# A 31-tap depthwise convolution: from VectorE to TensorE, 4 taps x 32 channels in the rows, 4 groups in the columns

## The chip, the cores and the metric

One core of a Trainium2 chip runs the whole program in one launch. The metric is the time of one execution on the device, in microseconds (us). The kernel before takes 3641.28 us (median of 3 runs, 3637.17 to 3642.21).

## The reference, cut to what matters

Two layers (`DEPTH = 2`) work on 1024 latent and 256 context tokens of width 1024. In each, one input projection feeds four mixers of 256 channels: a recurrence (RG-LRU), attention, a convolution module and hyena, a pair of long convolutions. One output projection joins them, and a mixture of 32 experts follows. In the last layer context tokens feed only the recurrence and the attention, so the convolution module runs on 1280 tokens in layer 0 and on 1024 in layer 1. The convolution module is:

```
def conformer_conv(pc, conv_w, conv_b, ln_g, ln_b, w_pw, b_pw):
    u = pc[..., :W_C] * jax.nn.sigmoid(pc[..., W_C:])               # W_C = 256 channels
    u = dwconv(u, conv_w, conv_b, (CONF_K // 2, CONF_K // 2))       # CONF_K = 31 taps, one filter per channel
    u = layer_norm(u, ln_g, ln_b)
    return jax.nn.silu(u) @ w_pw + b_pw
```

`dwconv` is depthwise: output channel c at time t is the sum over j of w[j, c] u[t + j - 15, c], plus a bias. All of it is in float32.

## The kernel before

Every layer has the same stages. What bears on this change is in two of them.

**Stage 1 (`phase1`).** Channels lie on the 128 partitions, tokens along the row. `win` makes one block of 128 projected columns: 24 products of 128 x 512 (or 256) per group of tokens, from a high and a low part of weights and inputs (L1065). The weights come over one buffer `wir` and are split by ScalarE (L948) and GpSimd (L951). The order is: the input of the first half of the recurrence, the recurrence on it (`recur(0)`), the two blocks of the convolution module (`glu_evac`), the recurrence's gate, `recur(1)`, then queries, keys and values, and the second gate. The recurrence goes piece by piece, 6 pieces for each half: GpSimd and VectorE make a 4-tap convolution `rg_u` (L1399, then three instructions of L1401), TensorE two products from it (L1404, four instructions), ScalarE, VectorE and GpSimd the gates, and VectorE a scan (L1421, L1424). `rg_u` has one buffer, so a piece starts when the one before has let it go (L1411).

Queries and keys leave as high and low parts: `qk_evac` issues 4 stores for each of 12 tiles in layer 0 (fewer in layer 1) to `qkd` in DRAM (L1087). The attention loads them back (L1269, L1276).

`conv31` is called after all of these. Its input is `cu`, a tile [128, 1309] per block of 128 channels with 15 zeros around the tokens; one `tensor_scalar` (L1446) and 30 `scalar_tensor_tensor` (L1448) go over it, one per tap, on VectorE, and a store (L1449) puts the result `cacc` into `cd` in DRAM. There are two blocks per layer, 120 instructions of L1448 in all. The same two `cu` buffers later take weights of the next layer's modulation (layer 0, L976).

**Stage 2 (the convolution module's rest and hyena).** When stage 1 has given its memory back, `hyena_in` loads six blocks of 128 channels (`hx`, L1717 and L1719), convolves them with 3 taps (`hu`, L1724 on GpSimd, L1727 on VectorE) and transposes them (L1734). `hyena` makes the long convolutions: a forward transform, a product with a spectrum, an inverse transform, twice; TensorE multiplies with tables `tabc` that stream from DRAM (L1661, L1771), VectorE does the rest. `conformer` loads 512 tokens of `cd` per step (`cx`, L1470), takes the mean with a product (L1473), the deviations with another (L1482), spreads them (L1457) and applies the pointwise product (L1495). The calls stand in this order: `hyena_in` of two blocks, hyena's first forward transform, the attention's transposes, `hyena_in` of four blocks, `conformer`, the rest of `hyena`.

**What sets the order.** The language's planner gives every engine and DMA queue one fixed order of instructions. It goes by its own costs: an engine takes, of the instructions that are ready, the one that stands first in the program's text, so what is traced late fills gaps. On the chip every engine follows that order and waits where an operand is late. All plain DMAs are issued by SyncE's one queue (SPq), in order, and a DMA that waits holds those behind it.

Of the kernel before, what the change touches and what calls it, by code (L numbers as in the profile page):

```python
# [13 lines left out]
def rope_tables():  # L14
    rows = SEQ // GRID_W
    row = np.repeat(np.arange(rows, dtype=np.float32), GRID_W)
    col = np.tile(np.arange(GRID_W, dtype=np.float32), rows)
    inv = (np.float32(10000.0) ** (-np.arange(ROPE_FREQS, dtype=np.float32) / np.float32(ROPE_FREQS))).astype(np.float32)
    ang = np.concatenate([row[:, None] * inv, col[:, None] * inv], -1).astype(np.float32)   # [L, 16]
    c, s = np.cos(ang).T, np.sin(ang).T  # L20
    cos = np.tile(np.concatenate([c, c], 0), (4, 1))
    sin = np.tile(np.concatenate([-s, s], 0), (4, 1))
    return np.stack([cos, sin]).astype(np.float32)      # [2, 128, L]


def feats(L):
# [5 lines left out]
    return np.ascontiguousarray(f.T), tu                # [33, L], [L]  # L32


# Long convolution over n = 2048 points, split by k = 8 q + r, t = 256 a + p.
# Slots of 128 frequencies: 0: r0 (q < 128), 1: r4, 2-3: r1, 4-5: r2, 6-7: r3.
SLOT_R = [(0, 0), (4, 0), (1, 0), (1, 1), (2, 0), (2, 1), (3, 0), (3, 1)]
# what the butterflies give: real part and imaginary part with a sign
# [3 lines left out]
class Bank:  # L42
# [11 lines left out]
    def array(self):  # L54
        return np.ascontiguousarray(np.stack(self.blocks, 1))    # [128, nb, 128]


def long_tables():
# [3 lines left out]
    plan_f = []          # per slot: (re list, im list) of (input, half, block)  # L62
    for s, (r, qb) in enumerate(SLOT_R):
        q = np.arange(128) + 128 * qb
        th = 2 * np.pi * np.outer(p, 8 * q + r) / n       # [p, q]
        C, S = np.cos(th), np.sin(th)
        re, im = [], []
        for h in range(2):
            sl = slice(h * 128, h * 128 + 128)
            if r == 0:  # L70
                re.append(("a0", h, fw.add(C[sl])))
                m = -S[sl].copy()
                m[:, 0] = np.cos(np.pi * p[sl])           # k = 1024 in the place of Im of k = 0
# [11 lines left out]
    plan_i = {}          # per output: per half: list of (part, slot, block)  # L85
# [27 lines left out]
def short_tables():  # L113
    """n = 512, 256 times: slots 0: k < 128 (and k = 256 in Im's first row), 1: 128 <= k < 256."""
# [31 lines left out]
def pieces(tabs, long):  # L146
    """The tables' blocks in the order of their use, 8 to a piece, and where each product finds its block."""
# [24 lines left out]
def conv_tables():  # L172
    """The long convolution's tables, each frequency group's complex products as three real ones, in pieces of 4
    blocks in the order of use: forward, then inverse. Per group its pieces, each with two lists of
    (input, half, block) or (input, slot, block)."""
# [34 lines left out]
    # inverse  # L210
# [10 lines left out]
    # R = C (Yr + Yi) - (C + S) Yi, I = C (Yr + Yi) + (S - C) Yr  # L221
# [7 lines left out]
    # the short ones  # L229
# [17 lines left out]
D = 1024  # L247
# [6 lines left out]
def bcast_rows(ap1d, n, parts=P):  # L254
    """A DRAM vector of n elements as [parts, n], each partition the same."""
# [3 lines left out]
def moe_consts(K, nfix):  # L259
# [13 lines left out]
    # column (f, i): i in the partitions of f, -1 in the others  # L273
# [11 lines left out]
    iota(d, [[1, P]], 0, -1)                        # col - part  # L285
    K.tri = c.tile([P, P], BF, name="tri")          # tri[t', t] = t' < t
# [3 lines left out]
    K.half = c.tile([P, 1], FT, name="half")        # 1 in partitions 64 and up  # L290
# [8 lines left out]
class Router:  # L299
    """The lists of each step's tokens, from the logits of one block of tokens after the other.  # L300

    The first nfix steps take the experts of that number, the others the rest by falling count; step i has
    caps[i] rows, in blocks of 128 and, for up to 64, a last one of 64."""

    def __init__(self, K, l, NB, caps, nfix, keep, w, lists):
# [13 lines left out]
        self.cnt = keep.tile([P, 4, NE], BF, name="rcnt")       # of the rows so far, by partition  # L319
# [5 lines left out]
    def first_max(self, x, n, oh, neg):  # L325
        """One-hot oh of the first of x's largest, whose negative goes to neg"""
# [9 lines left out]
    def choose(self, b, lg):  # L336
        """The two experts of a block's tokens and their gates"""
# [9 lines left out]
        # logits of the chosen group  # L347
# [25 lines left out]
    def place(self, b):  # L373
        """A block's assignments into the lists [(value, expert), rank]"""
# [3 lines left out]
        # ranks: the rows above in the block and those of the blocks before  # L378
# [24 lines left out]
    def finish(self):  # L403
# [9 lines left out]
        # each expert's position, and the permutation  # L413
# [11 lines left out]
        # the lists as they are, and the first 64 rows of each block twice  # L425
# [11 lines left out]
        # 2**20 in rows of no assignment; half rows in blocks of 64, the first half in the lower partitions  # L437
# [6 lines left out]
        # the order of the experts last: the first rows are wanted ahead of more weights  # L444
# [11 lines left out]
    def beyond(self):  # L456
        """Whether any expert has more rows than its step"""
# [1855 lines left out]
```

## Time and profile before

| | |
|---|---|
| time, median of 3 runs | 3641.28 us (3637.17 to 3642.21) |
| span of the profiled execution, first to last instruction | 3627.2 us |
| what lies around the span (median less span) | 14.1 us |
| TensorE (PE) busy | 3060.8 us, 84% |
| VectorE (DVE) busy | 2269.4 us, 63% |
| ScalarE (ACT) busy | 1564.9 us, 43% |
| GpSimd (POOL) busy | 717.3 us, 20% |
| the 31 taps (L1448, 120 instructions) | 194.3 us of DVE |

The span is the profiled execution's own time; no other time of it is given. Rows that list groups of instructions read: line, engine, operation, output<-inputs, shapes, count | busy us, mean ns of one | idle time of the engine just before them and what ended it. A matrix product of 32-bit floats is recorded as two MATMUL instructions. DMA share is the mean busy share of the core's 16 DMA engines, PEclk the granted TensorE clock as a share of 2.4 GHz.

### The profile page before, as it was taken

Reading aid. Unit: us, or ns where it says so; the run is one execution under the profiler, and the core shown is the slowest. Engines: PE = TensorE matmul, PEld = TensorE weight load, DVE = VectorE, ACT = ScalarE, POOL = GpSimd, SP = SyncE. Lnnn points to the kernel's source line nnn. Section 1 sums busy time; section 2 is a strip of 40 time slices with the busy share of each in tenths; the row PEclk is TensorE's granted clock in tenths of the full one; section 3 lists DMA queues with packets and bytes.
Section 4 is the critical chain, followed back from the end, with each engine's and each line's share of the span. In section 5 each row is a group of like instructions: output and inputs, shape, how many; then the busy total and the mean of one; then the engine's idle time right before and its main releaser. Section 6 shows DMA issues by size and latency. Waiting matters only on the chain. (4 is left out here: it accounts for less than half of the span.)

```text
span 3627.2 us, 43878 instructions
## 1 busy us (share of the span) xinstructions
PE 3060.8 (84%) x14952; PEld 2066.6 (57%) x14952; DVE 2269.4 (63%) x3297; ACT 1564.9 (43%) x2537; POOL 717.3 (20%) x579
## 2 busy tenths in 40 slices
PE   5898775998789699999998587789888799899993
PEld 1246664676568354577554465557667665465552
DVE  6675873887768444375543678478886753356626
ACT  4234342774324233365543454267433344345523
POOL 2213441001320101111110444300230111111102
PEclk9999987999999699999999798889989899999996
DMA  6751224223566789996978512221446389978796
GB/s 189 225 196 49 69 85 159 81 73 128 168 197 218 241 299 325 355 327 235 319 259 329 176 38 93 83 83 65 151 152 216 130 300 372 384 276 292 267 348 246
DMA packets 415023, 743.33 MB, mean 205 GB/s; under 512 B 45867, under 2 KB 180888, under 8 KB 414794
## 3 DMA queue, kind: packets, MB, share of 16 engines
q1 hardware_dynamic: 397194, 702.69, 55.8%
q0 software_dynamic: 17600, 37.79, 3.1%
q8 instruction: 119, 1.95, 0.2%
q14 instruction: 110, 0.90, 0.1%
HBM read 656.13 MB, written 105.30 MB: 210 GB/s over the span
## 5 line engine op out<-in xcount | busy, mean ns | idle before, releaser
L679 DVE TENSOR_TENSOR wl<-wr,wh 128x1024 fp32r<-128x1024 f32 (+1 forms) x440 | 516.2, 1202 | 392.0 <-ACT wh L678 379.4
L678 ACT ACTIVATE wh<-wr 128x1024 fp32r<-128x1024 f32 (+1 forms) x440 | 442.2, 1038 | 328.7 <-PE mm L730 190.7
L1065 PE MATMUL mm<-hh,wih 128*128 128x512 f32 (+1 forms) x752 | 292.6, 390 | 51.5 <-ACT stg L1126 39.6
L734 PE MATMUL mm<-wr,xl 128*64 128x512 f32 x1216 | 328.0, 609 | 4.2 <-DVE xl L690 1.6
L1065 PE MATMUL mm<-hh,wil 128*128 128x512 f32 (+1 forms) x752 | 290.6, 387 | 18.0 <-POOL wil L951 17.4
L730 PE MATMUL mm<-wh,xh 128*128 128x512 f32 x704 | 289.5, 412 | 6.7 <-ACT wh L678 6.2
L1065 PE MATMUL mm<-hl,wih 128*128 128x512 f32 (+1 forms) x752 | 290.9, 387 | 1.5 <-DVE hl L951 0.9
L730 PE MATMUL mm<-wl,xh 128*128 128x512 f32 x704 | 278.3, 395 | 3.6 <-DVE wl L679 3.5
L730 PE MATMUL mm<-wh,xl 128*128 128x512 f32 x704 | 277.1, 394 | 0.0
L790 POOL DMA_INDIRECT fd<-ot,ridx x82 | 94.5, 1152 | 839.7 <-ACT ot L786 262.0
L1448 DVE SCALAR_TENSOR_TENSOR cacc<-cu,cw,cacc 128x1295 f32<-128x1295 f32 (+1 forms) x120 | 194.3, 1619 | 1.9
L1065 PEld LDWEIGHTS mm<-hh,wih 128*128 128x128 f32 x752 | 147.5, 196 | 83.1 <-ACT stg L1126 43.2
L671 POOL DMA_INDIRECT gb<-h2d,ridx x82 | 98.8, 1205 | 462.6 <-PE tr L698 192.7
L730 PEld LDWEIGHTS mm<-wh,xh 128*128 128x128 f32 x704 | 133.4, 190 | 92.6 <-issue 45.1
L1196 DVE TENSOR_REDUCE m<-A 128x1 f32<-128x1024 f32 x128 | 156.1, 1220 | 44.0 <-PE A L1186 36.8
L951 POOL TENSOR_TENSOR wil<-wir,wih 128x1024 fp32r<-128x1024 f32 x34 | 91.4, 2688 | 465.4 <-ACT wih L948 409.4
L734 PEld LDWEIGHTS mm<-wr,xl 128*64 128x64 f32 x1216 | 96.0, 137 | 141.7 <-issue 126.7
L1065 PEld LDWEIGHTS mm<-hh,wil 128*128 128x128 f32 x752 | 147.4, 196 | 48.5 <-POOL wil L951 20.0
L1065 PEld LDWEIGHTS mm<-hl,wih 128*128 128x128 f32 x752 | 148.2, 197 | 31.3 <-issue 6.0
L780 PE MATMUL mm<-wr,hl 128*64 128x512 f32 x608 | 153.9, 602 | 0.0
L730 PEld LDWEIGHTS mm<-wl,xh 128*128 128x128 f32 x704 | 133.8, 190 | 30.6 <-DVE wl L679 6.6
L1241 ACT ACTIVATE wT<-TR 128x512 f32<-128x512 f32 (+1 forms) x200 | 104.9, 524 | 107.0 <-PE TR L1236 97.7
(491 smaller groups left out, 6493.0 us busy)
## 6 DMA issues: line engine op xcount, KB each, us to landing
wr<-in_moe_w_gate_dram SPq DMA_DIRECT2D x256, 512.0 KB
wr<-in_moe_w_up_dram SPq DMA_DIRECT2D x256, 512.0 KB
wr<-in_moe_w_down_dram SPq DMA_DIRECT2D x256, 512.0 KB
wada<-in_w_ada_dram SPq DMA_DIRECT2D x48, 512.0 KB
tabc<-in_k_t_c_dram SPq DMA_DIRECT2D x88, 256.0 KB
wir<-in_w_in_dram SPq DMA_DIRECT2D x40, 512.0 KB
wr<-in_w_ada_dram SPq DMA_DIRECT2D x32, 512.0 KB
ks<-qkd SPq DMA_DIRECT2D x16, 640.0 KB
```

The costliest lines, as they stand in the source:

```text
L671: self.K.nc.gpsimd.indirect_dma_start(out=g[s, :D // (1 + h)], out_offset=None, in_=self.h2d[h], in_offset=bass.IndirectOffsetOnAxis(ap=id ...
L678: nc.scalar.activation(hi, src, AF.Copy)
L679: nc.vector.tensor_tensor(lo, src, hi.bitcast(FT), op=OP.subtract)
L730: nc.tensor.matmul(ps[b][w], x(k), y[:, kk], start=(k == 0 and c == 0), stop=(k == 7 and c == 2))
L734: nc.tensor.matmul(ps[b][0][w * 64:(w + 1) * 64], self.XT[n0 + b](k), raw[w][:, kk], start=(k == 0), stop=(k == 7))
L780: nc.tensor.matmul(po[b][0][o * 64:(o + 1) * 64], HT[b][:, k], raw[:, o], start=(k == 0), stop=(k == 3))
L790: s = nc.gpsimd.indirect_dma_start(out=self.fd[h], out_offset=bass.IndirectOffsetOnAxis(ap=ridx[r], axis=0), in_=ot[r], in_offset=None, bo ...
L951: (eng or nc.vector).tensor_tensor(lo, src, hi.bitcast(FT), op=OP.subtract)
L1065: nc.tensor.matmul(p[:, :n], a[:, k], b[:, k, t0:t0 + n], start=(k == 0 and a is wh and b is hh), stop=(k == 7 and a is wl))
L1196: nc.vector.tensor_reduce(m[:, c, 1:2], A[c], axis=AX.X, op=OP.max, negate=True)
L1241: nc.scalar.activation(o, i_, AF.Copy)
L1448: nc.vector.scalar_tensor_tensor(a, u[:, j:j + N], cw(j), a, op0=OP.mult, op1=OP.add)
```

## The change

The 31 taps move out of stage 1 into `conformer`, onto TensorE. Channels are taken in groups of 32. A product has 4 taps x 32 channels in its 128 rows: the right operand holds 32 channels in four copies, each shifted by one token, the left one the diagonals of four taps' weights. Eight such products add up 31 taps (the 32nd is zero). Four groups of channels write to four different quarters of the output's partitions, so four products stand side by side in the array's columns.

- `glu_evac` works in its `stg` tile and stores it to `ud` in DRAM (6 stores in layer 0, 4 in layer 1); `stg` has 3 buffers instead of 2, in every place that uses it. The zeros around the tokens are written to `ud` once, at the start.
- `taps` is new, at the head of stage 2: 8 small loads of weights, a transpose, and one VectorE instruction of 128 x 2048 that makes the diagonals.
- `conv31` is called by `conformer` in place of the load of `cd`: per 512 (or 256) tokens and block of 128 channels it issues 4 loads (32 partitions x 4 groups x 540 or 284 floats each), 32 products and one ScalarE instruction that adds the bias. There are 6 such calls in layer 0 and 4 in layer 1.
- Gone: `cu` and its zeros, `cacc`, `cd`, its 4 stores and 10 loads; the `cu` tiles that take modulation weights are now 1024 wide and nothing uses them before.

```
-                        u = wd.tile([P, N], FT, name="cu", bufs=2)
-                        ...
-                        self.win(l, w, [12 + b, 10 + b], hs, allg, self.glu_evac(wd, u))
+                        self.win(l, w, [12 + b, 10 + b], hs, allg, self.glu_evac(wd, b))
-                for b in range(2):
-                    self.conv31(l, wd, b, us[b], ctx_out)
     def glu_evac(self, w, b):
...
-            nc.vector.scalar_tensor_tensor(u[:, o:o + n], th[0][:, :n], 1.0, p[:, :n], op0=OP.add, op1=OP.mult)
+            t = th[0][:, :n]
+            nc.vector.scalar_tensor_tensor(t, t, 1.0, p[:, :n], op0=OP.add, op1=OP.mult)
+            nc.sync.dma_start(self.ud[b * P:(b + 1) * P, o:o + n], t)
-    def conv31(self, l, w, b, u, ctx_out):
-        a = w.tile([P, N], FT, name="cacc")
-        nc.vector.tensor_scalar(a, u[:, 0:N], cw(0), self.pc("c_conv_b", b), op0=OP.mult, op1=OP.add)
-        for j in range(1, 31):
-            nc.vector.scalar_tensor_tensor(a, u[:, j:j + N], cw(j), a, op0=OP.mult, op1=OP.add)
-        nc.sync.dma_start(self.cd[b * P:(b + 1) * P, :N], a)
+    def taps(self, l, w, wr):
+        R = wr.tile([64, 4, 32], FT, name="taps", bufs=1)
+        nc.gpsimd.memset(R, 0.0)
+        for j in range(8):
+            m = min(4, 31 - 4 * j)
+            nc.sync.dma_start(R[j * 8:(j + 1) * 8, :m],
+                              bass.AP(tensor=cw.tensor, offset=cw.offset + 4 * j * 256, ap=[[32, 8], [256, m], [1, 32]]))
+        p = self.pr.tile([P, 512], FT, name="rg")
+        nc.tensor.transpose(p[:, :64], R.rearrange("r s c -> r (s c)"), self.ident[:64, :64])
+        t = wr.tile([P, 64], FT, name="tapsT", bufs=1)
+        nc.scalar.activation(t, p[:, :64], AF.Copy, scale=0.5)
+        one = wr.tile([P, 32], FT, name="tap1", bufs=1)
+        nc.vector.tensor_reduce(one, self.ident.rearrange("p (s c) -> p c s", s=4), axis=AX.X, op=OP.add)
+        W = w.tile([P, 64, 32], FT, name="tapw", bufs=1)
+        nc.vector.tensor_tensor(W, one[:, None, :].to_broadcast([P, 64, 32]), t[:, :, None].to_broadcast([P, 64, 32]),
+                                op=OP.mult)
+        return W
+    def conv31(self, w, b, W, out, o, n):
+        x = w.tile([P, 4, 540], FT, name="cr4", bufs=2)
+        u = self.ud[b * P:(b + 1) * P].rearrange("(g c) t -> c g t", g=4)
+        for s in range(4):
+            nc.sync.dma_start(x[s * 32:(s + 1) * 32, :, :n + 28], u[:, :, o + s:o + s + n + 28])
+        p = self.pr.tile([P, 512], FT, name="rg")
+        for j in range(8):
+            for g in range(4):
+                nc.tensor.matmul(p[g * 32:(g + 1) * 32, :n], W[:, j * 8 + b * 4 + g], x[:, g, 4 * j:4 * j + n],
+                                 start=(j == 0), stop=(j == 7))
+        nc.scalar.activation(out, p[:, :n], AF.Identity, bias=self.pc("c_conv_b", b))
     def conformer(self, l, w, ctx_out, W):
...
-                nc.sync.dma_start(acc[:, b, :n], self.cd[b * P:(b + 1) * P, o:o + n])
+                self.conv31(w, b, W, acc[:, b, :n], o, n)
...
+                    W = self.taps(l, w, hc)
                     for b in range(2):
                         self.hyena_in(l, hc, b, ut, ctx_out)
```

The rest of the diff takes out comments.

## Rows read from the trace of the kernel before

**Rows 1.** The page: span, and part 1, busy time of each engine.
```profile
span 3627.2 us, 43878 instructions
...
PE 3060.8 (84%) x14952; PEld 2066.6 (57%) x14952; DVE 2269.4 (63%) x3297; ACT 1564.9 (43%) x2537; POOL 717.3 (20%) x579
```

**Rows 2.** The page, part 5: the costliest groups; the taps, and a 1024-wide DVE operation.
```profile
L679 DVE TENSOR_TENSOR wl<-wr,wh 128x1024 fp32r<-128x1024 f32 (+1 forms) x440 | 516.2, 1202 | 392.0 <-ACT wh L678 379.4
...
L1448 DVE SCALAR_TENSOR_TENSOR cacc<-cu,cw,cacc 128x1295 f32<-128x1295 f32 (+1 forms) x120 | 194.3, 1619 | 1.9
```

**Rows 3.** Windows: stretch, length, busy us of PE, PEld, DVE, ACT, POOL; PEclk, DMA share, GB/s.
```profile
290.00:336.00 46.00, 38.27 (x173) 29.16 (x172) 18.99 (x25) 24.67 (x34) 16.05 (x14) 0.93 0.12 35
336.00:540.00 204.00, 157.86 (x811) 129.93 (x811) 174.24 (x145) 74.93 (x99) 93.70 (x54) 0.89 0.22 69
...
867.00:937.00 70.00, 43.08 (x193) 36.31 (x192) 54.08 (x54) 13.80 (x27) 38.91 (x38) 0.78 0.76 248
937.00:982.00 45.00, 41.63 (x182) 30.76 (x180) 26.87 (x46) 19.57 (x27) 3.43 (x2) 1.00 0.37 109
...
2086.00:2121.00 35.00, 28.95 (x114) 22.11 (x113) 21.79 (x28) 19.88 (x27) 15.18 (x12) 0.95 0.17 48
2121.00:2300.00 179.00, 142.54 (x678) 113.68 (x677) 157.47 (x142) 76.78 (x99) 83.86 (x52) 0.89 0.19 62
...
2588.00:2642.00 54.00, 39.18 (x173) 33.12 (x174) 50.74 (x58) 12.15 (x22) 28.21 (x25) 0.81 0.70 227
2642.00:2682.00 40.00, 33.76 (x128) 22.44 (x128) 24.35 (x40) 13.87 (x18) 4.39 (x3) 0.87 0.25 82
```

**Rows 4.** Windows of line L1448 alone, 336 to 540 us.
```profile
336.00:540.00 204.00, 102.29 (x60) 0.89 0.22 69
```

**Rows 5.** The same, 2121 to 2300 us.
```profile
2121.00:2300.00 179.00, 91.25 (x60) 0.89 0.19 62
```

**Rows 6.** Waits of PE, 290 to 336 us: us in total, times, longest.
```profile
PE rg L1404 <- DVE rg_u L1401: 6.3, 3, 4.4
```

**Rows 7.** Waits of PE, 336 to 540 us.
```profile
PE rg L1404 <- DVE rg_u L1401: 37.2, 8, 14.8
```

**Rows 8.** Waits of PE, 2086 to 2121 us.
```profile
PE rg L1404 <- DVE rg_u L1401: 3.6, 1, 3.6
```

**Rows 9.** Waits of PE, 2121 to 2300 us.
```profile
PE rg L1404 <- DVE rg_u L1401: 39.6, 9, 8.3
```

**Rows 10.** Timeline of SyncE's queue, layer 0: start, us, line, DMA, count.
```profile
350.67 1.11 SPq L1387 DMA_DIRECT2D gw<-in_a_w_r_dram  x2
...
437.30 1.48 SPq L1087 DMA_DIRECT2D qkd<-qhi  x2
...
494.53 1.35 SPq L1087 DMA_DIRECT2D qkd<-qlo  x1
...
533.56 1.08 SPq L1087 DMA_DIRECT2D qkd<-qhi  x2
...
581.63 2.33 SPq L1087 DMA_DIRECT2D qkd<-qlo  x1
```

**Rows 11.** DMA, 533 to 584 us.
```profile
DMA packets 3642, 5.19 MB, mean 102 GB/s; under 512 B 93, under 2 KB 1630, under 8 KB 3640
```

**Rows 12.** Timeline of PE, 2 to 100 us: products in four column groups.
```profile
57.27 0.61 PE L979 MATMUL mp<-wada,sT 128*2 128x256 f32 x8
...
69.64 1.04 PE L979 MATMUL mp<-wada,sT 128*2 128x256 f32 x14
```

**Rows 13.** Timeline of PE, 858 to 1003 us: full-width products of 512 columns.
```profile
952.26 1.88 PE L1473 MATMUL rg<-cx,om 128*128 128x512 f32 x4
```

**Rows 14.** Waits of PE, 867 to 937 us.
```profile
PE rg L1734 <- DVE hu L1727: 25.8, 5, 10.6
```

**Rows 15.** Waits of PE, 2588 to 2642 us.
```profile
PE rg L1734 <- DVE hu L1727: 13.9, 4, 6.7
```

More of the change, by code (lines that the diff above doesn't have):

```diff
@@ L855 @@
 C8 = math.sqrt(0.5)
+UW = T0 + 46
 GROUPS = [(0, 512, 0), (512, 512, 0), (1024, 256, 1)]
@@ L908, in setup @@
         self.yd = self.dram.tile([8, P, T0], FT, name="yd")
-        self.cd = self.dram.tile([2 * P, T0 + 15], FT, name="cd")
+        self.ud = self.dram.tile([2 * P, UW], FT, name="ud")
+        z = c.tile([P, 2, 16], FT, name="zeros")
+        nc.vector.memset(z, 0.0)
+        for o, n in ((0, 15), (15 + TL, 15), (30 + T0, 16)):
+            nc.sync.dma_start(self.ud[:, o:o + n].rearrange("(b p) t -> p b t", p=P), z[:, :, :n])
     def params(self, l, psum, R):
@@ L917, in params @@
         for n, cnt in (("a_conv_w", 16), ("a_conv_b", 4), ("a_b_r", 4), ("a_b_i", 4), ("a_lam", 4),
-                       ("c_conv_w", 62), ("c_conv_b", 2), ("c_ln_g", 2), ("c_ln_b", 2), ("c_b_pw", 2),
+                       ("c_conv_b", 2), ("c_ln_g", 2), ("c_ln_b", 2), ("c_b_pw", 2),
                        ("d_conv_w", 18), ("d_conv_b", 6)):
@@ L1106, in win_v, with glu_evac @@
             nc.scalar.activation(vt[:, b:b + 2].rearrange("p b c -> p (b c)"), p, AF.Copy)
-    def glu_evac(self, w, u):
+    def glu_evac(self, w, b):
         nc, th = self.nc, []
         def f(p, t0, n, v):
-            th[:] = [w.tile([P, 512], FT, name="stg", bufs=2)]
+            th[:] = [w.tile([P, 512], FT, name="stg", bufs=3)]
             nc.scalar.activation(th[0][:, :n], p[:, :n], AF.Tanh, scale=0.5)
@@ L1124, in f @@
         def f(p, t0, n, v):
-            q = w.tile([P, 512], FT, name="stg", bufs=2)
+            q = w.tile([P, 512], FT, name="stg", bufs=3)
             nc.scalar.activation(q[:, :n], p[:, :n], AF.Copy)
@@ L1433, in f @@
         def f(p, t0, n, v):
-            g = w.tile([P, 512], FT, name="stg", bufs=2)[:, :n]
+            g = w.tile([P, 512], FT, name="stg", bufs=3)[:, :n]
             nc.scalar.activation(g, p[:, :n], AF.Gelu_apprx_tanh)
@@ L1438, in rglru_out @@
         return f
-    def conv31(self, l, w, b, u, ctx_out):
+    def taps(self, l, w, wr):
         nc = self.nc
-        N = TL + (15 + TC if ctx_out else 0)
-        a = w.tile([P, N], FT, name="cacc")
-        cw = lambda j: self.cw[:, j * 2 + b:j * 2 + b + 1]
-        nc.vector.tensor_scalar(a, u[:, 0:N], cw(0), self.pc("c_conv_b", b), op0=OP.mult, op1=OP.add)
-        for j in range(1, 31):
-            nc.vector.scalar_tensor_tensor(a, u[:, j:j + N], cw(j), a, op0=OP.mult, op1=OP.add)
-        nc.sync.dma_start(self.cd[b * P:(b + 1) * P, :N], a)
+        cw = self.I["c_conv_w"][l]
+        R = wr.tile([64, 4, 32], FT, name="taps", bufs=1)
[15 more added lines that the diff above has]
+    def conv31(self, w, b, W, out, o, n):
+        nc = self.nc
+        x = w.tile([P, 4, 540], FT, name="cr4", bufs=2)
[8 more added lines that the diff above has]
+        nc.scalar.activation(out, p[:, :n], AF.Identity, bias=self.pc("c_conv_b", b))
     def spread(self, p, r, t):
@@ L1458, in spread, with conformer @@
         return p
-    def conformer(self, l, w, ctx_out):
+    def conformer(self, l, w, ctx_out, W):
         nc, I = self.nc, self.I
@@ L2043, in phase1 @@
                 wd = self.pool(c, "wd")
-                self.cw = self.keep.tile([P, 62], FT, name="cw")
-                a = self.col["c_conv_w"]
-                nc.vector.tensor_scalar(self.cw, self.pp[:, a:a + 62], 0.5, None, op0=OP.mult)
-                N = TL + 30 + (15 + TC if ctx_out else 0)
-                us = []
                 self.pr = self.pool(c2, "r_ps", 3, space=PSUM)
@@ L2064, in phase1 @@
                     for b in range(2):
-                        u = wd.tile([P, N], FT, name="cu", bufs=2)
-                        nc.gpsimd.memset(u[:, 0:15], 0.0)
-                        nc.gpsimd.memset(u[:, 15 + TL:30 + TL], 0.0)
-                        if ctx_out:
-                            nc.gpsimd.memset(u[:, N - 15:N], 0.0)
-                        self.win(l, w, [12 + b, 10 + b], hs, allg, self.glu_evac(wd, u))
-                        us.append(u)
+                        self.win(l, w, [12 + b, 10 + b], hs, allg, self.glu_evac(wd, b))
                     gate(0, h)
@@ L2103, in phase1 @@
                     t = [lambda: xap.tile([P, T0 + 9], FT, name="xa")] + \
-                        [lambda: wd.tile([P, N], FT, name="cu", bufs=2)] * 2
+                        [lambda: wd.tile([P, D], FT, name="cu", bufs=2)] * 2
                     self.modulation(1, LATER, self.psum_mm, self.pool(c2, "mod"), t)
@@ L2170, in run @@
                         self.hyena_in(l, hc, b, ut, ctx_out)
-                    self.conformer(l, w, ctx_out)
+                    self.conformer(l, w, ctx_out, W)
                 wop = ExitStack()
```

## The prediction, made before the changed kernel was run

> **What bounds the kernel now.** I read the page first, then the taps' own line, the windows, PE's waits in each stretch, and SyncE's queue. The page shows TensorE busy for 84% of the 3627.2 us span and VectorE for 63% [rows 1]. By these shares alone one would not move work from DVE to PE; but a share is a mean over stages, and the change takes from one stage and gives to another.
>
> The taps are 120 instructions, 194.3 us of DVE [rows 2]. They run from 336 to 540 us in layer 0 and from 2121 to 2300 in layer 1, where DVE is busy 85% (174.24 of 204) and 88% (157.47 of 179) [rows 3]; 102.29 and 91.25 us of that are taps [rows 4, 5]. DVE is no longer idle enough there to answer at once, and PE stands 46.1 us (204 - 157.86) and 36.5 us (179 - 142.54). The waits say on what: the recurrence's products wait for `rg_u`, which DVE makes in three instructions that queue among 1.6 us taps: 37.2 us in 8 waits, and 39.6, of which 3.6 began before the taps, so 36.0 in 8 [rows 7, 9]. Just before, with no tap on DVE but one, PE waits 6.3 us for four pieces and 3.6 for four: 9.9 / 8 = 1.24 us each against 73.2 / 16 = 4.58 [rows 6, 8]. So in this stage the taps are on the path, through DVE's order.
>
> In stage 2 the picture is the reverse. While `hyena_in` runs (867 to 937, 2588 to 2642), DVE sets the pace (54.08 of 70, 50.74 of 54 busy) and PE waits 25.8 and 13.9 us for `hu` [rows 14, 15]. From 937 to 982 and 2642 to 2682 PE does (41.63 of 45, 33.76 of 40) and DVE has room [rows 3].
>
> **Taps out of stage 1.** Two ways to size it. By waits: if each of 16 pieces waits 1.24 us again, PE wins 73.2 - 19.8 = 53 us. By PE's pace: busy time times granted clock is work; with taps 157.86 x 0.89 / 204 = 0.689 and 142.54 x 0.89 / 179 = 0.709 per us, just before 38.27 x 0.93 / 46 = 0.774 and 28.95 x 0.95 / 35 = 0.786 [rows 3]. At the earlier pace the stretches last 181.5 and 161.4 us: 22 + 18 = 40 us less. I take the middle, -47. Ends: all of PE's idle time, -83, and nothing, 0.
>
> What is late next is the stream of query and key stores. It begins at 437.30 and its last store is issued at 581.63, with a hole from 496 (494.53 + 1.35) to 533.56 [rows 10]; in its last part it moves 102 GB/s at 5.19 MB in 51 us [rows 11]. In layer 0 it carries 10.5 MB (1280 tokens x 128 rows x 4 bytes x 4 copies x 4 blocks), 103 us at that rate, and spans 147. Up to 44 us of holes can close; my layer-0 share (47 x 204 / 383 = 25) fits. What comes behind its end stays as it is. The 10 stores to `ud` (256 KB or less) add some 2.4 MB to a stretch whose DMA share is 0.22 [rows 3], and as many bytes of `cd` stores go: 0, at most +2.
>
> **Products into stage 2.** A full-width product is two instructions, at 512 columns about 0.43 us apart (x4 in 1.88 us) [rows 13], so 0.86 us. In four column groups, eight instructions of 256 columns (four products) take 0.61 us and fourteen 1.04, so a further round costs 0.43 us [rows 12], as one full-width product of 256 columns would (half of 0.86): the four groups run side by side. At 512 columns a round is 0.86, and a call (8 rounds) 6.9 us; at 256, 3.4. Layer 0: 4 x 6.9 + 2 x 3.4 = 34.4; layer 1: 4 x 6.9 = 27.6; 62 us in all.
>
> Cover: PE's waits for `hu`, less the first one of layer 0 (10.6 us), when weights and inputs of the taps are still on their way: 15.2 us; in layer 1 some 8 of 13.9, and 4 of the 6.2 us that PE idles from 2642 to 2682. Left on PE's path 19.2 + 15.6 = 35 us. Without cover it is 62, with every gap used 10.
>
> The page "TensorE: Matmul & The Clock Gate" of the Trainium skill, Part 3, table of measured speedups, gives 3.07x for four row tiles and says that column tiles behave alike. By that figure the 62 us would be 81 and the sum 19 us worse (an estimate from that page). The round of 0.43 us contradicts it: measured, the ratio is 4.
>
> **Loads and small work.** `taps` puts 8 small loads into SyncE's queue ahead of `hx`; two like them take 1.1 us to issue [rows 10], so 4.4 us per layer. Its DVE instruction is 2048 wide; a 1024-wide one takes 1.2 us [rows 2], so 2.4, while DVE waits for `hx` anyhow. I take +5 for both layers together; ends 0 and +14. The 40 loads of `x` bring 10.0 MB (1.1 per call of 512 tokens), 2.4 MB of `cd` loads go. In 867 to 937 the engines are 0.76 busy at 248 GB/s, so 326 at the most; 17.4 MB are moved there, and 5.6 more, less the 4 loads of `cd` there (1.0), make 22.0 MB, 67 of the 70 us. It fits, barely: 0, at most +15 for both layers where a table `tabc` comes late behind them. The bound from the other side is the query stores' 102 GB/s: 10.8 us per call, longer than its products.
>
> The page "DMA: Bandwidth & Descriptors" of the Trainium skill, section on semaphore increments ("How many engines"), says that a transfer's slowest dimension sets how many engines carry it. The query stores lead with 4 and keep the share near a quarter, as the rows show; the loads of `x` lead with 32 and should use all. No run here shows that yet.
>
> The ten bias instructions (0.6 us each on ACT, busy 13.80 of 70) cost nothing; if ACT were late they would add 6. The three stores of zeros at the start: 0, at most +2. That everything behind is planned anew can be worth some us in either direction.
>
> **Sum.** -47 + 35 + 5 = -7. The span becomes 3620; with the 14.1 us that lie around it in the median (3641.28 - 3627.2), 3634.
>
> **Rivals.**
> - *Stage 2 hides it.* The planner puts the calls into all of PE's gaps, `hu`'s first one and those behind 982 included. For it: DVE sets the pace in 867 to 937; against: the calls stand ahead of hyena's rest, so they are taken before the later gaps. -53 + 10 + 5 = -38: 3603.
> - *Slower: PE takes the whole load in stage 2.* Place: PE's fixed order from `hyena_in` on. The loads of `x` have two buffers and stand in SyncE's queue between tables; if they land late, calls come not in the gaps but in front of hyena's products, when PE is the bound. For it: the DMA share of 0.76 and PE's 0.93 busy in 937 to 982. Against: the inputs lie in DRAM since stage 1. Price: 62 + 9 instead of 40, with -47: +24, 3665. It decides from the point where over 42 of the 62 us are not covered.
> - *The query stores keep stage 1 where it is.* The stream needs its ring of buffers and its 4 stores per tile, and its end does not move with PE's waits. For it: the last 48 us are stores without a hole; against: the hole before it lies where PE waits for `rg_u`. Gain 20 in place of 47: +20, 3661.
> - *The change does not do what it says:* the four groups overlap in part or not at all. Serial products cost 4 x 62 = 248, +179, 3820. Read with its end, half of the fourteen's 1.04 us is 0.52 us per round [rows 12]: 75 in place of 62, +13 - 7 = +6, 3647. The table cited above is the page's case for such a part overlap.
>
> **How the numbers follow.** A measurement of this kernel can tell 0.2%, 7.3 us, from no change. Forecast 0.42, own range 3616 to 3652; hidden 0.23; PE takes all 0.21; stores hold 0.11; overlap in part 0.02, none 0.01. Faster by over 0.2% (below 3634.0): half of the forecast's own cases and all of the hidden ones, 0.21 + 0.23 = 0.44. Within: 0.16 of the forecast and 0.05 of the stores and PE cases at their mild ends, 0.21. Slower: the rest, 0.05 + 0.18 + 0.09 + 0.03 = 0.35. The range is 3596 to 3671: it takes in the hidden case with a margin and both slower ones.
>
> **What would show it.** Right: no tap on DVE in stage 1 and DVE busy near 35 to 45% there; PE's waits for `rg_u` near 1.2 us a piece; the hole in the query stores shorter and the attention 20 to 30 us earlier in layer 0; products of four groups in rounds of 0.86 us; stage 2 longer by some 20 us in each layer. Wrong: rounds over 1 us; `rg_u` waits that stay (then the taps were not their cause); PE waiting for `x` or more for `tabc`; or an attention that starts no earlier.

## The result and the profile after

| | before | after |
|---|---|---|
| time, median of 4 runs each, side by side | 3639.23 us (3636.11 to 3642.21) | 3697.48 us (3690.62 to 3703.65) |
| ratio, 95% interval | | 1.0165 (1.0141 to 1.0189) |

The change makes the kernel 1.65% slower, some 60 us; 3634 was predicted, and the range ended at 3671. Ratios here are made from undisturbed runs only, so they need not be the quotient of the medians beside them.

The page after, span and part 1; they answer to [rows 1]:

```profile
span 3697.0 us, 45181 instructions
...
PE 3126.5 (85%) x15594; PEld 2079.5 (56%) x15594; DVE 2071.1 (56%) x3176; ACT 1570.2 (42%) x2548; POOL 676.4 (18%) x571
```

VectorE lost the 194.3 us of [rows 2] and a little more, TensorE gained 65.7. The spans are 69.8 us apart and the medians 58. In all executions whose span is on record the time is 1.8 to 2.3 us longer than the span, so the 14.1 us that the table before the prediction puts around it are no fixed part of the time: the profiled execution of the kernel before was probably some 12 us quicker than the median. The stages tell where the 69.8 us are. Let stage 1 run from the first product of `win` to the attention's first score product, and stage 2 from the last product of `win` to the first of the output projection. Windows of the kernel before, stages 1 and 2 of layer 0, then of layer 1 (columns as in [rows 3]):

```profile
275.70:610.70 335.00, 248.21 (x1225) 201.57 (x1223) 206.46 (x192) 114.99 (x157) 124.86 (x88) 0.88 0.25 84
867.10:1055.00 187.90, 140.39 (x602) 113.43 (x600) 138.93 (x175) 49.15 (x74) 71.15 (x76) 0.88 0.57 183
2034.30:2366.90 332.60, 245.82 (x1113) 195.65 (x1113) 221.20 (x226) 133.18 (x191) 138.09 (x90) 0.85 0.26 89
2579.60:2746.20 166.60, 124.83 (x544) 97.53 (x543) 134.87 (x171) 47.82 (x71) 59.84 (x67) 0.87 0.53 170
```

The same four of the changed kernel, and a stretch of 50 us in its second one:

```profile
278.40:586.60 308.20, 245.42 (x1225) 199.60 (x1224) 96.52 (x130) 114.66 (x157) 103.69 (x82) 0.90 0.27 91
844.20:1091.00 246.80, 179.51 (x987) 126.50 (x985) 139.42 (x177) 53.32 (x81) 71.07 (x77) 0.85 0.53 157
2073.60:2386.00 312.40, 238.70 (x1112) 191.07 (x1112) 132.12 (x164) 131.66 (x190) 121.29 (x90) 0.88 0.28 95
2599.40:2816.20 216.80, 151.10 (x802) 103.36 (x801) 137.00 (x173) 51.00 (x76) 58.02 (x68) 0.84 0.50 147
914.00:964.70 50.70, 43.88 (x300) 15.67 (x300) 3.44 (x6) 9.71 (x14) 0.00 (x0) 0.87 0.38 100
```

Stage 1 is 26.8 and 20.2 us shorter, 47 in all, as predicted. Stage 2 is 58.9 and 50.2 us longer, 109 in all, where 40 were predicted. All other stages together differ by 8 us. Each length is that of one execution; how far they can be trusted is seen from kernels of the table below that share a stage: fourteen have the changed kernel's stage 1, 615.2 to 624.3 us for both layers, and four have the stage 2 of before, 350.3 to 354.5. TensorE's busy time in stage 2 grew by 39.1 and 26.3 us, so about 44 us of the loss are not its work at all. The last window shows where the other engines are then: TensorE is busy, VectorE for 3.44 of 50.7 us.

The products cost what was worked out. PE's groups of their line in the changed kernel, by shape:

```profile
L1484 PE MATMUL rg<-cr,tapw 128*32 128x512 f32 x512 | 56.9, 602 | 0.0
L1484 PE MATMUL rg<-cr,tapw 128*32 128x256 f32 x128 | 7.1, 380 | 0.0
```

That is 64.0 us for 62. PE's timeline of the changed kernel, layer 0 (start, length, line, operation, count, idle time before):

```profile
913.85 2.37 PE L1771 MATMUL rg<-ident,hu 128*128 128x128 f32 x10 [5.21 <-DVE hu L1764]
916.15 14.33 PE L1484 MATMUL rg<-cr,tapw 128*32 128x512 f32 x128
930.40 2.01 PE L1510 MATMUL rg<-cx,om 128*128 128x512 f32 x4
934.88 1.95 PE L1519 MATMUL rg<-om,csq 128*128 128x1 f32 x16 [2.47 <-ACT csq L1514]
938.21 2.04 PE L1494 MATMUL rg<-cr,ones_f 128*128 128x512 f32 x2 [1.38 <-DVE cr L1491]
943.22 5.91 PE L1532 MATMUL rg<-cx,wpw 128*128 128x512 f32 x8 [2.97 <-ACT cx L1527]
949.06 13.94 PE L1484 MATMUL rg<-cr,tapw 128*32 128x512 f32 x128
962.93 2.00 PE L1510 MATMUL rg<-cx,om 128*128 128x512 f32 x4
964.77 0.59 PE L1808 MATMUL mm<-Yl,tabc 128*128 128x256 f32 x2
```

The first call stands behind the last transposes of `hu`, so it fills none of their waits. Then two steps of the conformer run bare, with short idle times between their products, and only at 964.77 does hyena's inverse go on (`Yl`), the work that would have kept VectorE busy. Why so late? SyncE's queue in the same stretch:

```profile
896.30 35.97 SPq L1480 DMA_DIRECT2D cr<-ud  x14
947.75 2.47 SPq L1536 DMA_DIRECT2D yd<-cy  x2
950.27 1.86 SPq L1698 DMA_DIRECT2D tabc<-in_k_t_c_dram  x4
952.18 0.43 SPq L1698 DMA_DIRECT2D tab<-in_k_t_s_dram  x1
```

The loads of the third and fourth `x` are the last eight of a group of 14 at which the queue stands for 36 us. Behind them come the output stores of the conformer's first step (`yd`), for which it stands again until 947.75, and only then the inverse's tables, issued at 950.27. The queue's waits over stage 2 of layer 0 (us in total, times, longest), and VectorE's, below, the other end of the chain:

```profile
SPq L1698 <- PE mm L1808: 56.8, 36, 8.3
SPq L1480 <- PE rg L1484: 33.8, 4, 20.2
...
SPq L1536 <- ACT cy L1535: 20.9, 6, 15.4
```

```profile
DVE cx L1513 <- PE rg L1510: 53.3, 3, 23.4
```

The tables' wait for their own buffers (the first row) is no sign of the loss: it was 55.0 us in the kernel before. The loads' wait (the second row) is new, and the stores' (the third) was 10.7. `x` has two buffers; each load of a third waits for TensorE to finish a call, and TensorE reaches the calls late. VectorE stands 53.3 us before the conformer's deviations; in the kernel before these were 8.8 us in 2 waits.

### The profile page after: what moved, and what is told of

Its sections match the earlier page's. It is cut to its first block, busy times and chain, and to the rows that moved or that the text cites. A ratio compares the mean times of both kernels' runs of the same rounds, so it can differ in the third digit from the quotient of the medians.

```text
span 3697.0 us, 45181 instructions
## 1 busy us (share of the span) xinstructions
PE 3126.5 (85%) x15594; PEld 2079.5 (56%) x15594; DVE 2071.1 (56%) x3176; ACT 1570.2 (42%) x2548; POOL 676.4 (18%) x571
## 5 line engine op out<-in xcount | busy, mean ns | idle before, releaser
L679 DVE TENSOR_TENSOR wl<-wr,wh 128x1024 fp32r<-128x1024 f32 (+1 forms) x440 | 516.4, 1203 | 390.3 <-ACT wh L678 382.7
L730 PEld LDWEIGHTS mm<-wh,xl 128*128 128x128 f32 x704 | 133.4, 189 | 28.8
```

Of the source, the lines that this page charges most:

```text
L679: nc.vector.tensor_tensor(lo, src, hi.bitcast(FT), op=OP.subtract)
L730: nc.tensor.matmul(ps[b][w], x(k), y[:, kk], start=(k == 0 and c == 0), stop=(k == 7 and c == 2))
```

## The experiments

Theories: **queue** (the loads of `x` wait for their buffers in SyncE's queue and hold hyena's tables), **order** (the calls stand in TensorE's order ahead of hyena's inverse and are paid there in full, whatever the queue does), **work** (64 us of products are too much for a stage that TensorE bounds). One table for all; "sum" is stage 2 of both layers. Kernels that leave products or taps out have other numbers in the experts' lists: between layer 0's experts and layer 1's first product e1, e2, e6 and e17 need 174 to 177 us instead of 46 to 50, so only their stages are read.

| kernel | median us | ratio to before (95%) | stage 1, layers 0, 1 | stage 2, layers 0, 1 | sum |
|---|---|---|---|---|---|
| before | 3639 | | 335.0, 332.6 | 187.9, 166.6 | 354.5 |
| after | 3697 | 1.0165 | 308.2, 312.4 | 246.8, 216.8 | 463.6 |
| e1 before, 1 tap | - | - | 307.0, 314.3 | 184.8, 165.5 | 350.3 |
| e2 one product | - | - | 308.6, 309.9 | 235.2, 205.4 | 440.6 |
| e3 inverse first | 3643 | 1.0025 (1.0011 to 1.0040) | 304.8, 310.6 | 219.9, 189.0 | 408.9 |
| e4 x on GpSimd | 3647 | 1.0035 (1.0022 to 1.0049) | 304.6, 310.6 | 217.9, 193.6 | 411.5 |
| e5 e3 and e4 | 3633 | 1.0000 (0.9987 to 1.0013) | 310.0, 311.2 | 216.8, 181.2 | 398.0 |
| e6 e4, one product | - | - | 305.9, 312.7 | 201.9, 173.4 | 375.3 |
| e7 before, inverse first | 3631 | 0.9993 (0.9980 to 1.0006) | 335.3, 334.0 | 180.4, 166.5 | 346.9 |
| e8 e4, conformer early | 3664 | 1.0082 (1.0055 to 1.0109) | 304.5, 312.2 | 235.9, 197.6 | 433.5 |
| e9 three x | 3705 | 1.0206 (1.0181 to 1.0232) | 305.4, 312.4 | 251.0, 220.8 | 471.8 |
| e10 e5, taps late | 3636 | 1.0010 (0.9997 to 1.0024) | 304.3, 312.4 | 218.6, 181.3 | 399.9 |
| e11 e10, forward first | 3680 | 1.0132 (1.0104 to 1.0159) | 304.7, 311.3 | 251.2, 203.7 | 454.9 |
| e12 e10, conformer last | 3740 | 1.0296 (1.0268 to 1.0324) | 309.9, 314.4 | 271.0, 237.6 | 508.6 |
| e13 half the taps | 3650 | 1.0026 (1.0014 to 1.0037) | 319.3, 323.4 | 203.8, 178.9 | 382.7 |
| e14 products in stage 1 | 3648 | 1.0030 (1.0017 to 1.0043) | 350.4, 337.5 | 185.2, 167.0 | 352.2 |
| e15 e5, x on ScalarE | 3646 | 1.0024 (1.0010 to 1.0039) | 304.0, 312.4 | 224.2, 191.1 | 415.3 |
| e16 loads in halves | 3706 | 1.0200 (1.0173 to 1.0227) | 305.0, 313.1 | 253.5, 223.7 | 477.2 |
| e17 e5, one product | - | - | 308.3, 310.1 | 205.7, 173.0 | 378.7 |
| e18 e14, earlier | 3651 | 1.0048 (1.0034 to 1.0062) | 344.9, 349.2 | 185.8, 166.9 | 352.7 |

**e1: stage 1 by itself.** `-for j in range(1, 31):` `+for j in range(1, 1):` in the kernel before's taps.

> The kernel before with only the first of the 31 taps (the 30 scalar_tensor_tensor left out): it prices stage 1 without anything added to stage 2. Theory (stage 1 gave what was forecast, all of the loss lies in stage 2): attention starts 25 to 30 us earlier in layer 0, about 22 in layer 1, stage 2 unchanged within 5 us; 3639 - 48 = 3591. Rival (the changed kernel's stage 1 gained from something else too, the stores to ud or the gone cd stream): less than 30 us in all, 3609 or more.

Stage 1 has the changed kernel's length to within 2 us, 307.0 and 314.3, and stage 2 is unchanged within 4. Stage 1's gain is the taps' absence; a gain from anything else is too small to be seen. The forecast of a total was useless, for the reason above.

**e2: the products.** `-for j in range(8):` `+for j in range(1):` in the changed kernel's `conv31`, with `start=True, stop=True` in the product.

> The changed kernel with one of the eight rounds per call (7 of 8 tap products left out; loads, weights and bias stay). It takes 7/8 of 64 us = 56 us of products off TensorE. Order theory (the calls stand in TensorE's order ahead of hyena's inverse and are paid in full, and VectorE idles meanwhile): stage 2 loses 56 us or a little more, 3697 - 56 = 3641 or less, but not all of the 109. Queue theory (the loads of x in SyncE's queue hold hyena's tables): the loads stay, so at least half of the loss stays, 3665 or more.

Only 23 us of stage 2's 109 go with 7/8 of the products. As the loads stay, this is the queue theory's answer. Stage 2 of layer 0 in e2, and the issue of the inverse's tables there:

```profile
847.30:1082.50 235.20, 155.99 (x650) 116.37 (x649) 141.48 (x177) 53.71 (x81) 69.67 (x77) 0.79 0.56 165
```

```profile
950.88 1.85 SPq L1698 DMA_DIRECT2D tabc<-in_k_t_c_dram  x4
```

The tables go out 104 us behind the stage's start (106 in the changed kernel), though 7/8 of the products ahead of them are gone. 31 us of products were taken out there (7/8 of 35.4), but TensorE's busy time fell by 23.5 (179.51 - 155.99): the granted clock fell from 0.85 to 0.79 on the mean.

**e3: order.** `+next(hy)` ahead of `self.conformer(...)`: hyena's first inverse is traced before the conformer.

> The changed kernel with hyena's first inverse traced ahead of the conformer (one next(hy) more before it), so that the inverse's products stand ahead of the calls in text order. Order theory: VectorE has the inverse's work while TensorE does the calls; stage 2 loses the 20 to 25 us per layer beyond the products' own time, and part of the products finds gaps: -35 to -60, about 3650. Queue theory: the loads of x still share one queue with the tables, whatever stands first; -10 at most, 3687 or more.

**e4: queue.** `-nc.sync.dma_start(x[...], ...)` `+nc.gpsimd.dma_start(x[...], ...)`.

> The changed kernel with the 40 loads of x issued by GpSimd's queue instead of SyncE's. Queue theory (third and fourth x wait in SyncE's queue for the two buffers, 20 to 34 us at a time, with hyena's tables behind them): the tables come early, -30 to -40, about 3660. Order theory: TensorE's order is the same, -10 at most, 3687 or more.

Each gives back about half, 55 and 52 us of 109. e3 came out as the order theory said and against the queue theory, e4 the other way round: neither holds as it was put. PE's timeline of e4 in the stretch that was shown above:

```profile
910.49 14.17 PE L1484 MATMUL rg<-cr,tapw 128*32 128x512 f32 x128
924.59 2.01 PE L1510 MATMUL rg<-cx,om 128*128 128x512 f32 x4
926.44 2.75 PE L1808 MATMUL mm<-Yl,tabc 128*128 128x256 f32 x12
929.07 1.95 PE L1519 MATMUL rg<-om,csq 128*128 128x1 f32 x16
930.87 1.97 PE L1808 MATMUL mm<-Ysum,tabc 128*128 128x256 f32 x8
```

The text of e4 has the calls where the changed kernel has them, yet hyena's inverse (`Yl`, `Ysum`) now stands between the conformer's products and fills their waits. By the planner's rule (it takes, of what is ready, what stands first in the text) this follows if it reckons with earlier tables; its own times are not on record. In e4 the queue is the only edit, so there the tables' place in SyncE's queue is the cause, and TensorE's order follows from it. e3 says that it is the place and not the wait. These are its waits for `x`'s buffers in layer 0, little less than the 33.8 us above, and the issue of the inverse's last tables:

```profile
SPq L1480 <- PE rg L1484: 27.4, 4, 13.4
```

```profile
920.65 0.85 SPq L1698 DMA_DIRECT2D tabc<-in_k_t_c_dram  x2
```

The tables are out before the queue stands at the third `x`, 80 us behind the stage's start, and TensorE does the inverse before the first call. How much of e3's gain is the tables' place and how much the products' order was not taken apart. Every such edit replans what comes after, so 52 us is what the queue's change is worth with all that it moves.

**e5: both.**

> Both single edits together: hyena's first inverse traced ahead of the conformer, and the loads of x in GpSimd's queue. If both edits cured the same thing (the hold in SyncE's queue, which e3 avoids by putting the inverse's tables ahead of the loads), they don't add up: within 10 us of 3643 to 3647. If they cured two things (order of the products, and the queue), they add up: 3690 - 54 - 50, about 3600.

398.0: 66 us of the 109, not the 107 that two causes would have given. They cure mostly the same thing. The kernel stands level with the one before.

**e6: e4 and e2 together.**

> One of the eight rounds per call (7 of 8 tap products left out), with the loads of x in GpSimd's queue. Only stage 2 is read, as what is left out changes the experts' lists. With the queue free, what is left of stage 2's growth (30 us in layer 0, 27 in layer 1 against the kernel before) should be the products' own time, 35 and 29 us: stage 2 comes back to 188 to 193 and 167 to 172 us. If something else holds it (the extra loads' traffic, the late conformer), it stays over 205 and 182.

From e4 to e6 the sum falls by 36 us, to 375.3, between the two answers. In layer 0 TensorE is busy for 7.4 us more than in the kernel before, but the stage is 14 us longer:

```profile
843.70:1045.60 201.90, 147.80 (x650) 112.99 (x649) 141.24 (x177) 53.27 (x81) 82.38 (x101) 0.85 0.65 192
```

**e7: control**, the edit of e3 in the kernel before.

> Control: the kernel before with hyena's first inverse traced ahead of the conformer and nothing else. Queue theory: nothing in the kernel before waits in SyncE's queue for the conformer's buffers for long, so the order alone gains nothing: within 8 us of before. Order theory: the order is good for itself, 15 us or more faster.

No change in the total; stage 2 7.5 us shorter in layer 0, 0.1 in layer 1. So the order of e3 is not good for itself; it cures what the change brought.

**e8: the conformer traced ahead of the last four `hyena_in`**, with e4's queue.

> The loads of x in GpSimd's queue, and the conformer traced ahead of the last four hyena_in instead of behind them, so that its products stand first in text order and can fill TensorE's waits for hu (25 us in layer 0, 24 in layer 1 in the changed kernel). If cover is to be had there as the prediction thought: stage 2 shorter by another 15 to 25 us per layer than with the queue alone, 3647 - 30 to 3647 - 50, about 3605. If the loads of x come too late for it or VectorE becomes the bound: no gain over 3647.

22 us worse than e4, and TensorE's waits for `hu` are as long, 15.8 and 13.8 us for 15.4 and 12.7. They were not the cover that the prediction took them for.

**e9 and e16: the wait or the number of loads.** e9: `name="cr4", bufs=3`. e16: each load in two halves, `for g in (0, 2): ... x[..., g:g + 2, ...]`.

> The changed kernel with three buffers for x instead of two, loads still in SyncE's queue. If it is the wait for x's buffers that holds the tables in that queue: one call more is loaded ahead, and of the 52 us that GpSimd's queue gave back in both layers a good part comes, 15 to 40 us: 3660 to 3680. If it is only that the 40 loads cost the queue their issue time (0.45 us each, 18 us): no gain, 3690 to 3700.

> The changed kernel with every load of x cut into two of half the size: 80 loads instead of 40 in SyncE's queue, the same bytes, the same two buffers, the same order. If the number of loads is what the queue loses (52 us for 40): 20 us or more slower than the changed kernel, 3717 or more. If the wait for x's buffers is (the loads stand there anyway until TensorE is through): within 10 us of it, 3687 to 3707.

A third buffer gives nothing (sum +8), against the queue theory as it was put; but twice the loads cost little (sum +14; total 3706 for 3697, as forecast for the wait). The row of e16 that answers to the 35.97 us above, 27 loads in place of 14:

```profile
892.16 38.56 SPq L1481 DMA_DIRECT2D cr<-ud  x27
```

So the number of loads is at most a small part: 40 more in this queue cost 14 us, 40 fewer (e4) gave 52 back. SyncE's queue in e9 shows why a third buffer does not help:

```profile
890.71 29.59 SPq L1480 DMA_DIRECT2D cr<-ud  x14
944.11 2.06 SPq L1536 DMA_DIRECT2D yd<-cy  x2
946.26 7.61 SPq L1480 DMA_DIRECT2D cr<-ud  x8
953.91 1.85 SPq L1698 DMA_DIRECT2D tabc<-in_k_t_c_dram  x4
```

The 14 loads are through 7 us sooner behind the stage's start than in the changed kernel. Then the queue stands at the stores of the conformer's first step, which starts no earlier, eight more loads follow, and the tables go out 9 us later. One buffer more moves the hold and does not end it. Buffers for all six calls were not tried.

**e10 to e12: later still.** e10: `self.taps(...)` behind the first two `hyena_in`. e11 and e12: two and three `next(hy)` ahead of the conformer, otherwise as e10.

> Both edits of e5 (inverse first, x in GpSimd's queue), and the tap weights traced behind the first two hyena_in instead of ahead of them. In e5 TensorE's first product of stage 2 in layer 0 is the taps' transpose, and it waits 9.7 us, with hu's transposes behind it. If that wait is paid: stage 2 of layer 0 5 to 10 us shorter than e5's 216.8, layer 1 0 to 5: about 3623. If hu would be waited for just as long anyhow: within 3 us of e5.

> As e10, with hyena's second forward transform traced ahead of the conformer too, so that its products only take what gaps are left. If gaps are there to be filled (TensorE is busy for some 170 of the 217 us in e5): 10 to 30 us better than e10 over both layers, about 3600 to 3615. If the conformer then comes too late and its chain (mean, deviation, pointwise product, store, load for the output projection) ends stage 2: as e10 or up to 20 us slower.

> As e11, with all of hyena but its last transposes traced ahead of the conformer. Same two answers: gaps filled best of all (3590 to 3610), or the conformer's chain stands at the end of stage 2 and costs what its last step takes (some 20 us per layer): 3640 or more.

The wait for the taps' weights hid behind `hu`'s: in layer 0 TensorE's waits for `hu` are 22.6 us where e5 has 15.2 and 9.7 for the weights, and nothing is gained. With the conformer later its chain ends the stage, 55 and 109 us worse, more than was expected for e11: in layer 0 of both TensorE waits 34.4 and 33.0 us for the output projection's input at the end, a wait that e10 does not have. e5's place is the best of those tried.

**e13: half.** The first block's taps stay on VectorE, the second block goes to TensorE, with e5's edits.

> Half of the change: the first block of 128 channels keeps its 31 taps on VectorE in stage 1, the second goes to TensorE in stage 2, with x in GpSimd's queue and hyena's inverse first as in e5. If stage 1's loss is proportional to the taps (24 us back of 48) and stage 2's too (half of the 44 us that e5 leaves), the sum stays near e5 and before: 3630 to 3640. If half the taps fit into VectorE's idle time of stage 1, and half the products into TensorE's of stage 2 (each loss sets in only behind a slack): 3600 to 3615.

Stage 1 gives 22 us back, half of 47; stage 2 is 28 above before, two thirds of e5's 43.5, and the total is above both forecasts. Neither stage has slack that a smaller load would fit into.

**e14 and e18: the products in stage 1.** `conv31` is called there in pieces of 256 tokens and stores `cd`, and stage 2 is that of before; in e14 behind `recur(1)` with loads in SyncE's queue, in e18 ahead of it with GpSimd's.

> The products stay in stage 1, where the taps stood, behind the recurrence's second half and ahead of queries and keys, 256 tokens at a time, loads in SyncE's queue; stage 2 is that of the kernel before (cd stored and loaded again). Stage 2 should come back to 188 and 167 us. Stage 1 of the changed kernel is 308 and 312 us, of which TensorE idles 63 and 74. If the products fill that: under 320 us each, total 3600 to 3615. If they stand in front of it in TensorE's order and are paid in full: 308 + 36 and 312 + 29, total 3650.

> As e14 (products in stage 1, stage 2 as before), but ahead of the recurrence's second half, where no query store is under way, and with x in GpSimd's queue. In e14 the query stores had a hole from 472.9 to 543.8 us in which SyncE's queue held x's loads and cd's stores. If that hole is what made stage 1 of e14 42 and 25 us longer: 15 to 25 us per layer less, about 3610. If the products are paid in full on TensorE (36 and 29 us): as e14, 3640 to 3650.

Stage 2 comes back to 185 and 167 us, and stage 1 pays more than in full: 67 us (687.9 - 620.6) for 65.5 us of products in e14, 73 in e18. In e14 the query stores have a hole:

```profile
472.91 1.35 SPq L1094 DMA_DIRECT2D qkd<-qlo  x1
...
543.82 1.09 SPq L1094 DMA_DIRECT2D qkd<-qhi  x2
```

In e18 the calls run from 383 to 447 us and the stores' hole is 41.5 us, from 503.3 to 544.7, not far from the 32 of the changed kernel; yet it is no faster, as the whole stream of stores runs later. So the hole is not what was paid: the products are.

**e15: ScalarE's queue** in place of GpSimd's in e5.

> As e5 with the loads of x in ScalarE's queue instead of GpSimd's. If e5 still loses to GpSimd waiting for x's buffers (19.6 us in layer 0, with hyena's products of that engine behind it): 5 to 15 us faster than e5. If ScalarE, which empties TensorE's results, is held by the same wait: 5 to 20 us slower.

17 us more stage 2 than e5, so ScalarE's queue is the worse place. That its emptying of TensorE's results is held up was the theory; it was not followed in the trace.

**e17: e5 and e2 together.**

> e5 (inverse first, x in GpSimd's queue) with one of the eight rounds per call (7 of 8 tap products left out). Only stage 2 is read, as what is left out changes the experts' lists. If the products are paid at about the rate of e4 to e6 (36 of 56 us): 199 and 162 us, 37 less than e5's 216.8 and 181.2 together. If e5's order hides them: 210 and 178.

19 us of 56 come back, between the two answers, so e5's order hides up to two thirds of the products; part of what did not come back is clock, 0.83 for 0.88 in layer 0. But 24 us remain over before with nearly no product left.

## Why the prediction was wrong

- **Stage 1, right in size, half right in how.** -47 against -47.0 measured. That it fits to the microsecond is luck: -47 was the middle of two estimates, 53 and 40, and the fourteen kernels with this stage 1 give 43 to 52. The estimate of 53 took it from PE's waits for `rg_u` alone, 73.2 us falling to 19.8. PE's waits in the changed kernel, from 290 to 486 us and from 2120 to 2292, which answer to [rows 6 to 9]:

```profile
PE rg L1412 <- DVE rg_u L1409: 33.6, 11, 7.5
...
PE rg L1412 <- DVE rg_u L1409: 27.6, 10, 8.7
```

  The four of before add up to 86.7, so 25.5 us are gone, not 53; a piece still waits 2.6 us (61.2 / 24; 3.6 before). The rest is 13.7 us of layer 0's waits for split weights, ended by ScalarE and GpSimd (18.2 us before, 4.5 after), and 9.9 us of TensorE's busy time in both layers, for as many products at a granted clock of 0.90 and 0.88 instead of 0.88 and 0.85. The estimate by TensorE's pace (40 us) had all of this in it; the one by a named wait did not. The query stores behave as said: their hole, 37.7 us in [rows 10], is now 32.1, and the last store is issued 23.5 us earlier:

```profile
476.15 1.45 SPq L1093 DMA_DIRECT2D qkd<-qlo  x1
509.68 1.07 SPq L1093 DMA_DIRECT2D qkd<-qhi  x2
...
558.15 1.03 SPq L1093 DMA_DIRECT2D qkd<-qlo  x1
```

- **The products' time, right.** 64.0 us for 62, a round 0.87 us (13.94 / 16) for 0.86, and 0.44 (7.1 / 16) for 0.43 at 256 columns. The working of the last was loose: it took the six instructions between eight and fourteen [rows 12] for a round of eight. The part "Packing small matmuls" (Part 3) of the Trainium skill's page "TensorE: Matmul & The Clock Gate" would have made it 81 by its 3.07x (an estimate); the trace does not agree: four column groups cost what one full-width product does.
- **The cover, wrong in kind.** Of the 27 us 23 were to come from the waits for `hu`, and these are 24.1 and 24.3 us in stage 2 of the changed kernel (25.8 and 13.9 before): nothing was covered there. With the queue out of the way they shrink to 15.4 and 12.7 us, but in layer 0 it is hyena's inverse that stands in them (e4), and the calls come after the last `hu`. There 7/8 of the products cost 36 us of stage 2 (e4 to e6); that this is near the 35 forecast for all is luck, as the cover was to be another.
- **The step that failed: "The 40 loads of `x` ... 0, at most +15 for both layers where a table `tabc` comes late behind them".** It weighed bytes against the bandwidth left. The place in the queue was not weighed: the loads that wait for one of two buffers, and the conformer's stores behind them, hold every table that comes after; hyena's inverse then stands behind two steps of the conformer in TensorE's order, and VectorE idles. Measured: 52 us (e4), or 65 if the products go first (e2 to e6). The slower rival named this very place, but as a loss of cover, and priced it at 62 + 9; the hold itself was in no term, so its 3665 was short by 32 too.
- **Taps' weights and small work, +5.** With loads on GpSimd and 7/8 of the products out, 20.8 us remain over before (375.3 - 354.5). The last eighth of the products is at most 8 of it. The other 13 are open between the loads' traffic, the weights (e10: no gain from placing them later) and the new plan.

So 109 = 52 (queue) + 36 (7/8 of the products) + 21 (the rest), against 0 + 35 + 5. With queue and order mended, 47 won and 44 lost cancel, which is e5. No kernel here beats the one before; the best, e5, e7 and e10, cannot be told from it.

## What to carry to other kernels

Moving work to another engine moves its operands to a queue: for each new load ask what it waits for and what stands behind it in the same queue, not only whether the bytes fit. An order that looks like the cause may be a planner's answer to a late load, so try the load's queue and not the order alone. And idle time on an engine (48 and 42 us of TensorE's in stage 2 of the kernel before) is no cover unless the new work is ready in those gaps; how much it covers is seen by taking the work out of the changed kernel.

## What the runs showed of the hardware

- **GpSimd's instructions got shorter when VectorE's taps went.** Groups of GpSimd in stage 1 of layer 0, kernel before (line, shapes, count, then busy us and mean ns):

```profile
L1399 POOL TENSOR_SCALAR rg_u<-xa,pp 128x512 f32<-128x512 f32 x8 | 12.9, 1608 | 6.1 <-DVE rg_t L1411 6.1
...
L1409 POOL TENSOR_TENSOR rg_u<-rg_r 128x512 f32<-128x512 f32 x8 | 11.4, 1425 | 46.1 <-ACT rg_r L1408 25.8 <-ACT vt L1106 11.5 <-DVE rg_i L1406 8.9
```

  and in the kernel after:

```profile
L1417 POOL TENSOR_TENSOR rg_u<-rg_r 128x512 f32<-128x512 f32 x8 | 8.3, 1041 | 34.1 <-ACT rg_r L1416 34.1
L1407 POOL TENSOR_SCALAR rg_u<-xa,pp 128x512 f32<-128x512 f32 x8 | 6.2, 773 | 5.9 <-DVE rg_t L1419 5.9
```

  The same 8 instructions (`rg_u`, of L1399 and L1407) take 773 ns instead of 1608, and 770 in e1, where the taps alone are gone. The Trainium skill's page "SBUF — State Buffer", section "Who interferes with whom", says that a VectorE instruction with two inputs in SBUF contends with a GpSimd instruction that reads SBUF; the taps had two. The trace agrees. The `rg_u` chain begins with these instructions, so part of stage 1's gain may come this way; how much was not measured.
- **With less work TensorE's granted clock was lower.** In e2 it is 0.79 on the mean of stage 2 where the changed kernel has 0.85, a mean over its two levels of 1.2 and 2.4 GHz: 7.5 of the 31 us taken out were given back. The 16 product instructions of the conformer's L1532 with 512 columns, the same in both, take 945 ns each on the mean instead of 756. From e4 to e6 the clock fell likewise, from 0.90 to 0.85.
- **The loads of `x` use all DMA engines.** Two windows of e5 in which only such loads run (DMA share and GB/s at the end):

```profile
942.00:944.00 2.00, 2.00 (x24) 0.65 (x20) 2.00 (x5) 0.00 (x0) 0.25 (x1) 1.00 1.07 261
944.00:946.00 2.00, 2.00 (x25) 0.52 (x16) 1.21 (x3) 0.00 (x0) 0.00 (x0) 1.00 1.00 212
```

  The share of 16 engines is 1, for GpSimd's queue at least. The rule of the Trainium skill's page "DMA: Bandwidth & Descriptors" on how many engines carry a transfer, which the prediction cited, agrees. With all engines busy these loads move 212 to 261 GB/s here, under the 326 that the prediction took as the most.
